# A decoder trunk's attention stage: the order of TensorE's products written out by hand

## The chip, the cores and the metric

The kernel runs on one core of a Trainium2 chip. The metric is the device time of one execution in microseconds, as the median of several runs; less is better. The engines of the core work in parallel, each on its own queue of instructions and in the order of that queue: TensorE (PE; matrix products and transposes by a product with the identity), VectorE (DVE), ScalarE (ACT), GpSimd (POOL, which here also issues the gathers), and SyncE (SP), which issues other transfers.

## The reference

Two layers of a decoder: an mLSTM mixer, then multi-head latent attention, each followed by a SwiGLU block. It is computed for a prompt of 1,024 tokens and for 8 decode streams with one new token and 8,192 cached keys each. The change lies in the attention of the second layer:

```python
def mla_attend_prompt(q_lat, q_rope, c_kv, k_r):           # per block of queries, causal
    s = jnp.einsum('bqhc,bkc->bhqk', ql, c_kv) + jnp.einsum('bqhr,bkr->bhqk', qr, k_r)
    s = jnp.where(kpos[None, :] <= qpos[:, None], s * MLA_SCALE, -jnp.inf)
    p = jax.nn.softmax(s, axis=-1)
    return jnp.einsum('bhqk,bkc->bqhc', p, c_kv)

def mla_attend_sample(q_lat, q_rope, c_new, kr_new, cache_latent, cache_k_rope, page_table, layer_idx):
    def one_seq(args):                                     # per stream: all 8192 past keys and the new one
        c_all = jnp.concatenate([cache_latent[layer_idx, pages].reshape(past, KV_LORA), cn], axis=0)
        s = jnp.einsum('qhc,kc->hqk', ql, c_all) + jnp.einsum('qhr,kr->hqk', qr, kr_all)
        p = jax.nn.softmax(jnp.where(mask, s * MLA_SCALE, -jnp.inf), axis=-1)
        return jnp.einsum('hqk,kc->qhc', p, c_all)
```

There are 8 heads, 256 latent channels and 64 rotary ones; everything is float32, and the prompt's products are each made of three, from a high and a low part of both operands.

## The kernel before

**Prompt blocks and slots.** The prompt's attention is cut into 32 blocks, one per head `h` and group `G` of 256 queries; block (h, G) has 2G + 2 tiles of 128 keys, so `G` = 0 is short and `G` = 3 long. Block number 4h + i is a *slot* (i counts up to 3 in a head; odd heads but the last go through `G` from 3 down). In `prompt(h, G, ...)` TensorE makes two rows of scores `sc` (L1529 to L1536: three products with the keys `kt`, two with the rotary keys, a mask), DVE finds their maxima `mx` (L1537), ACT takes the exponentials into `px` (tag `wr`, L1546) and scales them by the reciprocal of their sum (L1551; from slot `LATE` on DVE does). Then TensorE *turns* the scaled tiles by products with the identity (L1567, into an `mm` bank), ACT and POOL split them into high and low parts `wh` and `wl` (L125 to L127, through a copy `spl`), the last turn of a block by ACT and DVE (L114, L115), and the *values* are the products with `vt` (L1587). `head_ops(h + 1)` makes the next head's `kt`, and for even heads the `vt` of two heads, a piece per slot (L131 to L133).

**Key halves.** The streams' cached keys come in 32 pieces of 2,048 keys; one is called a *half*, two make a unit, two units a stream. POOL gathers a half's latent rows into `nat` (four buffers, two gathers of 1 MB each) and its rotary rows into `nrp` (two buffers). DVE transposes them in five passes into `tt` (four buffers, L1684), and TensorE makes the stream's scores from each `tt`, 32 columns at a time (L1691; `qbd` holds the queries). After two halves comes the unit's softmax: maximum `rm` and bias `nb` on DVE, `al` and the exponentials `sS` on ACT (L1700, L1704), the running sum `lrow` and the transpose `pT` on DVE, sixteen copies of `pT` into `pz`, half on DVE and half on ACT (L1712), and the *stream sum* on TensorE, 32 products of `nat` by `pz` in the source, which read `nat` for the last time (L1716); `acc` takes it up. After a stream's second unit its *meeting* follows: ten small steps between DVE, TensorE and ACT that bring the keys' partial maxima and sums together (L1722 to L1741).

**What sets the order.** The source writes, slot by slot, a whole prompt block, a piece of `head_ops`, and one half (two in the slots `DBL`, none in `NONE`) from the generator `sample_units`. A scheduler then orders each engine's instructions by their priority, which is the place in the source, and by when it expects their operands; stream scores and sums are raised by `high_priority(offset=SOON)`. The queues' order is fixed when the program is built; at run time an engine only waits. `mmt(tag)` takes one of eight PSUM banks: four `sc`, two `mm`, two `ss`.

## Time and profile before

| | |
|---|---|
| median of 3 runs | 2774.49 us (2773.03 to 2780.6) |
| the profiled execution's own time | 2772.8 us |
| its span, first to last instruction | 2771.0 us |
| mean granted TensorE clock | 0.971 |
| busy: PE, DVE, ACT, POOL | 2594.2, 1497.7, 1177.0, 875.5 us |
| instructions in the profile | 52011 |

In the profile, lines as L1691 are those of the listing above. A group of instructions shows its busy time and the mean duration in ns, then the idle time of its engine just before, and what ended it. A row of waits shows who waited for whom, the total in us, the times and the longest. A float32 product shows as two PE instructions where the source has one. Slots 1 to 29 lie between about 1411 and 1907 us of the span, the stream work between 1435 and 1904.

### The profile page before, as it was taken

The numbers are of one execution on the slowest core, as the hardware profiler recorded it, in microseconds if no ns is written. First come the engines' busy times: TensorE is split into PE (matmuls) and PEld (weight loads), VectorE is DVE, ScalarE is ACT, GpSimd is POOL, SyncE is SP. The second block draws the span as 40 slices with busy tenths as digits, with TensorE's granted clock in tenths as the row PEclk, the third lists the DMA queues.
The fourth block names the chain that finished last, engine by engine and source line by source line (L and its number), as shares of the span: only waits on it lengthen the run. The fifth ranks groups of instructions, "written<-read, shape, count | busy, mean of one in ns | idle before, by whom it ended". The sixth has DMA issues, their size and how long they took to land. (4 is left out here: it accounts for less than half of the span.)

```text
span 2771.0 us, 52011 instructions
## 1 busy us (share of the span) xinstructions
PE 2594.2 (94%) x20719; PEld 2445.1 (88%) x20719; DVE 1497.7 (54%) x3217; ACT 1177.0 (42%) x2651; POOL 875.5 (32%) x843
## 2 busy tenths in 40 slices
PE   8999988989999999999878889898988999999998
PEld 8998877889999999998766677676888999999998
DVE  4345678853344333465547776677574444434445
ACT  4212334534444444443353455456344444444443
POOL 1001002243333333332243545442223333333333
PEclk9999999999999999999988999899999999999999
DMA  5133445326655656463566766653533655555553
GB/s 184 39 76 92 132 144 147 116 79 129 121 117 117 119 120 117 84 195 108 173 210 220 259 228 228 223 204 125 174 100 85 127 117 120 120 117 117 117 134 106
DMA packets 348905, 383.70 MB, mean 138 GB/s; under 512 B 26025, under 2 KB 300462, under 8 KB 340342
## 3 DMA queue, kind: packets, MB, share of 16 engines
q0 software_dynamic: 42064, 180.99, 27.7%
q1 hardware_dynamic: 279654, 182.83, 22.5%
q10 hardware_dynamic: 26944, 16.56, 2.3%
q8 instruction: 163, 2.67, 0.4%
q14 instruction: 80, 0.66, 0.1%
HBM read 254.58 MB, written 125.70 MB: 137 GB/s over the span
## 5 line engine op out<-in xcount | busy, mean ns | idle before, releaser
L131 PE MATMUL ss<-ah,dh 128*128 128x344 f32 x864 | 277.4, 321 | 6.6 <-ACT st L1075 6.2
L1075 ACT COPY st<-ss 128x344 f32<-128x344 f32 x432 | 189.9, 441 | 213.3 <-PE ss L133 180.4
L132 PE MATMUL ss<-al,dh 128*128 128x344 f32 x864 | 277.3, 321 | 1.9 <-POOL al L115 1.9
L133 PE MATMUL ss<-ah,dl 128*128 128x344 f32 x864 | 276.6, 320 | 0.0
L114 ACT ACTIVATE wh<-wr 128x512 fp32r<-128x512 f32 (+2 forms) x161 | 130.7, 812 | 238.7 <-PE mm L132 130.5
L1077 POOL DMA_DIRECT2D x_d<-st x144 | 124.3, 863 | 243.7 <-ACT st L1075 237.8
L131 PEld LDWEIGHTS ss<-ah,dh 128*128 128x128 f32 x864 | 163.0, 189 | 7.6 <-ACT st L1075 6.7
L132 PEld LDWEIGHTS ss<-al,dh 128*128 128x128 f32 x864 | 163.3, 189 | 2.4 <-POOL al L115 2.4
L115 POOL TENSOR_TENSOR al<-u,ah 128x512 fp32r<-128x512 f32 (+1 forms) x84 | 118.2, 1407 | 147.8 <-ACT ah L114 147.6
L1684 DVE STREAM_TRANSPOSE tt<-nat 128x1024 f32<-128x1024 f32 x128 | 153.8, 1223 | 18.9 <-PE ss L1691 13.8
L133 PEld LDWEIGHTS ss<-ah,dl 128*128 128x128 f32 x864 | 162.9, 189 | 0.0
L115 DVE TENSOR_TENSOR wl<-S,wl 128x512 fp32r<-128x512 f32 x89 | 77.4, 870 | 157.3 <-ACT wl L114 122.8
L115 DVE TENSOR_TENSOR wh<-S,wh 128x512 fp32r<-128x512 f32 x91 | 68.2, 750 | 121.5 <-ACT wh L114 93.1
L1041 DVE TENSOR_TENSOR u<-u,sc 128x260 f32<-128x260 f32 (+1 forms) x168 | 70.8, 422 | 115.0 <-PE sc L133 113.7
L115 DVE TENSOR_TENSOR wl<-wr,wh 128x1024 fp32r<-128x1024 f32 (+2 forms) x92 | 105.2, 1143 | 50.0 <-ACT wh L114 42.4
L1691 PE MATMUL ss<-tt,qbd 128*32 128x128 f32 x2560 | 99.0, 288 | 21.7 <-DVE tt L1684 12.8
L1007 POOL TENSOR_TENSOR S<-S,wr 128x512 f32<-128x512 f32 x45 | 62.9, 1397 | 175.8 <-DVE wl L115 87.9
L1000 POOL TENSOR_TENSOR S<-wr 128x512 f32<-128x512 f32 x45 | 61.6, 1369 | 163.4 <-DMA wr<-in_ffn_w_gate_up_dram 153.9
L1691 PEld LDWEIGHTS ss<-tt,qbd 128*32 128x32 f32 x2560 | 75.3, 114 | 40.4 <-DVE tt L1684 21.0
L131 PE MATMUL mm<-zh,wh 128*128 128x344 f32 x320 | 104.0, 325 | 7.2 <-DVE ot L459 7.2
L115 DVE TENSOR_TENSOR dl<-dr,dh 128x256 fp32r<-128x256 f32 x144 | 68.6, 476 | 72.9 <-ACT dh L114 72.9
L132 PE MATMUL mm<-zl,wh 128*128 128x344 f32 x320 | 103.2, 322 | 0.0
(917 smaller groups left out, 9275.8 us busy)
## 6 DMA issues: line engine op xcount, KB each, us to landing
x_d<-st POOLq DMA_DIRECT2D x144, 516.0 KB
wr<-in_ffn_w_gate_up_dram SPq DMA_DIRECT2D x98, 512.0 KB
dr<-in_ffn_w_down_dram SPq DMA_DIRECT2D x144, 128.0 KB
wr<-in_mlstm_w_in_dram SPq DMA_DIRECT2D x24, 512.0 KB
wr<-in_mlstm_w_out_dram SPq DMA_DIRECT2D x16, 512.0 KB
q<-qn_d SPq DMA_DIRECT2D x32, 256.0 KB
wr<-in_mla_w_o_dram SPq DMA_DIRECT2D x15, 512.0 KB
x_d<-x SPq DMA_DIRECT2D x16, 260.0 KB
```

What stands on the lines that cost most here:

```text
L114: ins = nc.scalar.activation(hi, src, AF.Copy)
L115: self.low = e.tensor_tensor(lo, src, hi.bitcast(F32), op=ALU.subtract)
L131: mm(ps, wh, xh, start=start, stop=False, **kw)
L132: mm(ps, wh, xl, start=False, stop=False, **kw)
L133: self.last = mm(ps, wl, xh, start=False, stop=stop, **kw)
L1000: G(s, a21, a22, op=ALU.add)
L1007: G(s, s, a11, op=ALU.subtract)
L1041: V.tensor_tensor(u[:, 1], u[:, 1], ps, op=ALU.add)
L1075: nc.scalar.copy(st[:, cs], ps)
L1077: nc.gpsimd.dma_start(self.x_d[:, d], st, accum_op=ALU.add)
L1684: V.transpose(out=tt, in_=src.rearrange("p s (c i) -> p c s i", i=32))
L1691: nc.tensor.matmul(psS[32 * j:32 * j + 32, u * P:u * P + P], self.qbd[:, b, cb], tt[:, c, 4 * j:4 * j + 4].rearrange("p s k -> p (s k)"), ...
```

## The change

The generator `sample_units`, the generator `head_ops` and the function `prompt` become objects with small steps: `Sample` (all streams), `Half` (one half), `Block` (one slot's prompt block). For slots 1 to 29 one loop writes the steps of both in a fixed pattern, and after the loop every TensorE instruction written in it gets a dependency on the TensorE instruction written before, without a semaphore: TensorE's queue is in the source's order. The other engines' queues are still the scheduler's. In the pattern of a slot:

- the *next* block's two rows of scores and their scaling are written in this slot (`nxt.scores`, `nxt.scale`), with this block's turns ahead and between them, two turns to a group, and its values at the end;
- a half's stream scores come in two groups, of three tiles at the slot's start and of two behind the next block's first scores; its transposes are written up to a half ahead;
- a unit's softmax is written at the end of its second half, its `pT` in the next half behind three transposes, its stream sum ahead of that slot's values; twelve of the sixteen `pz` copies are ACT's;
- a freed `nat` is gathered again right behind the sum (one now, one with the next half), `nrp` two halves ahead, and a block's `q` is loaded two slots ahead;
- a meeting's ten steps are spread as *hops* over the following halves, in the unit's own `ss` bank;
- the next head's keys and values are made in `sc` banks instead of `mm`; `DBL` is (4, 12, 20) and `NONE` is empty; `high_priority` is gone.

The core of the diff:

```diff
-NONE, DBL, LATE = (0, 31, 30), (3, 11, 27), 30
-SOON = 1000
+NONE, DBL, LATE = (), (4, 12, 20), 30
...
+    def probs(self):
+        if self.todo:
+            d = self.units[self.todo[0]]
+            if "pT" in d and not d.get("pz"):
+                for kb in range(4):
+                    for j in range(4):
+                        e = self.V.tensor_copy if kb == 3 else self.nc.scalar.copy
+                        e(self.k.pz[32 * kb:32 * kb + 32, j, :, 8 * kb:8 * kb + 8], d["pT"][32 * j:32 * j + 32, kb])
+                d["pz"] = True
+    def sums(self):
+        if not self.todo:
+            return False
+        U = self.todo[0]
+        d = self.units[U]
+        if not d.get("pz"):
+            return False
+        self.todo.pop(0)
+        nc, V = self.nc, self.V
+        psV = d["ss"][:, 256:512]
+        for i in range(8):
+            for j in range(4):
+                nc.tensor.matmul(psV[32 * j:32 * j + 32], self.k.pz[:, j, i], self.nat[2 * U + i // 4][:, j * 4 + i % 4], start=i == 0, stop=i == 7)
+        self.gather(2 * U + 4)
+        self.due = 2 * U + 5
+        self.add = lambda: V.scalar_tensor_tensor(d["q"]["acc"], d["q"]["acc"], d["al"], psV, op0=ALU.mult, op1=ALU.add)
+        return True
...
+    def soft(self, U):
+        nc, V, t = self.nc, self.V, self.t
+        d = self.units[U]
+        q = d["q"]
+        psS = d["ss"][:, 0:256]
+        rm = t([P, 1], "rm", 2)
+        V.reduce_max(rm, psS, axis=AX.X)
+        nb = t([P, 1], "nb", 3)
+        V.scalar_tensor_tensor(nb, rm, -SCALE, q["nb"], op0=ALU.mult, op1=ALU.min)
+        al = d["al"] = t([P, 1], "al", 2)
+        nc.scalar.activation(al, q["nb"], AF.Exp, bias=nb, scale=-1.0)
+        q["nb"] = nb
+        d["sS"] = t([P, 256], "sS", 1)
+        d["ls"] = t([P, 1], "ls", 2)
+        nc.scalar.activation(d["sS"], psS, AF.Exp, bias=nb, scale=SCALE, accum_out=d["ls"])
+        self.wait = U
+    def soft2(self, U):
+        V, t = self.V, self.t
+        d = self.units[U]
+        q = d["q"]
+        V.scalar_tensor_tensor(q["lrow"], q["lrow"], d["al"], d["ls"], op0=ALU.mult, op1=ALU.add)
+        d["pT"] = t([P, 4, 8, 8], "pT", 1)
+        V.transpose(out=d["pT"].rearrange("p k t h -> p t k h"), in_=d["sS"])
+        self.todo.append(U)
+        if U % 2:
+            self.meet(U)
...
+        s.scores(u, (1, 4, 0))
+        s.fetch()
+        s.turn(u, 2)
+        s.turn(u, 3)
+        s.turn(u + 1, 4)
+        s.late()
+        s.hop("V")
+    def second(self):
+        s, u = self.s, self.u
+        s.hop("P")
+        s.turn(u + 1, 0)
+        s.scores(u, (3, 2))
+        s.hop("V")
+    def third(self):
+        self.s.turn(self.u + 1, 1)
+    def fourth(self):
+        s, u = self.s, self.u
+        if u % 2:
+            s.soft(self.U)
+        s.rope(u + 2)
...
-            for i, G in enumerate(range(4) if h % 2 == 0 or h == 7 else range(3, -1, -1)):
-                slot = h * 4 + i
-                if slot >= early:
-                    prompt(h, G, cur["k"], vt)
-                next(gen, None)
-                if pr is None:
-                    pr = self.pr = self.pool("ma")
-                for _ in range(0 if slot in NONE else 2 if slot in DBL else 1):
-                    next(units)
...
+        for slot in range(1, 30):
+            h, i = divmod(slot, 4)
+            halves = [sam.take() for _ in range(0 if slot in NONE else 2 if slot in DBL else 1)]
+            u = halves[0] if halves else sam
+            far = Block(slot + 2)
+            far.load()
+            u.first()
+            ups = []
+            if h % 2 == 0 and h < 7:
+                if i == 0 and h > 0:
+                    ups = [lambda: make_v(h, 3, split_p, "sc"), lambda: load_uk(h + 1)]
+                if i == 2:
+                    ups = [lambda: make_k(h + 1, split_p, "sc"), lambda: load_uk(h + 2) if h < 6 else None]
+            elif h < 7:
+                if i == 0:
+                    ups = [lambda: make_k(h + 1, split_p, "sc"), lambda: load_uv(h + 1)]
+                else:
+                    ups = [lambda: make_v(h + 1, i - 1, split_p, "sc")]
+            turns = [lambda j=j: blk.turn(j) for j in range(0, blk.nk, 2)]
+            seq = turns[:2] + ups + turns[2:3] if full or not ups else ups + turns[:2]
+            rest = turns[len([x for x in seq if x in turns]):]
+            for f in seq:
+                f()
+            nxt.scores(0)
+            for f in rest[:1]:
+                f()
+            if len(halves) > 1:
+                sam.probs()
+                u.second()
+                for f in rest[1:]:
+                    f()
+                nxt.scale(0)
+                sam.sums()
+                u.third()
+                nxt.scores(1)
+                sam.hop("P")
+                u.fourth()
+                u = halves[1]
+                u.first()
+                sam.probs()
+                nxt.scale(1)
+                blk.values()
+                u.second()
+                full = sam.sums()
+            else:
+                sam.probs()
+                u.second()
+                for f in rest[1:]:
+                    f()
+                nxt.scale(0)
+                nxt.scores(1)
+                full = sam.sums()
+                nxt.scale(1)
+                blk.values()
+            u.third()
+            sam.hop("P")
+            u.fourth()
+            blk, nxt = nxt, far
...
+        traced = nc.cur_bb.bb.instructions
+        mark = traced[-1]
...
+        last = {}
+        for ins in traced[[k for k in range(len(traced)) if traced[k] is mark][-1] + 1:]:
+            e = ins.engine
+            if e == mybir.EngineType.PE and e in last:
+                self.tc.add_manual_dep(ins, last[e].name, mybir.DependencyInfo(mybir.DependencyClass.NoSync, mybir.DependencyReason.DATA), reason="order")
+            last[e] = ins
```

The order before and after, in slot 17 (head 4, `G` = 1, a block of four key tiles). On TensorE, before; `mm_18067` is a value tile of the next heads, `mm_18259` a turn of the slot's predecessor, `sc_18579` this block's scores, `ss_18300` the stream scores of a unit, `mm_18267` values:

```order
L132 MATMUL mm_18067<-swl_17699,ckh_13605 128x256
L133 MATMUL mm_18067<-swh_17697,ckl_13606 128x256
L1567 MATMUL mm_18259<-ct_66,wr_18238 128x128
L1567 MATMUL mm_18259<-ct_66,wr_18253 128x128 x2
L1529 MATMUL sc_18579<-kt_17555,q_18573 128x384
L1691 MATMUL ss_18300<-tt_18494,qbd_15149 32x128 x8
L1691 MATMUL ss_18300<-tt_18492,qbd_15149 32x128 x8
L1587 MATMUL mm_18267<-wh_18257,vt_16233 128x256
L1530 MATMUL sc_18579<-kt_17555,q_18573 128x384
L1531 MATMUL sc_18579<-kt_17555,q_18573 128x384
L1532 MATMUL sc_18579<-kk_13597,qrr_18574 128x384
```

After, from the same block's start; `ss_18547` holds stream scores, `mm_18586` and `mm_18595` are this block's two turns, and `sc_18605` the scores of slot 18:

```order
L143 MATMUL ss_18547<-tt_18526,qbd_15149 32x128 x8
L143 MATMUL ss_18547<-tt_18429,qbd_15149 32x128 x8
L143 MATMUL ss_18547<-tt_18479,qbd_15149 32x128 x8
L1832 MATMUL mm_18586<-ct_66,wr_18476 128x128
L1832 MATMUL mm_18586<-ct_66,wr_18512 128x128
L1832 MATMUL mm_18586<-ct_66,wr_18476 128x128
L1832 MATMUL mm_18586<-ct_66,wr_18512 128x128
L1832 MATMUL mm_18595<-ct_66,wr_18476 128x128
L1832 MATMUL mm_18595<-ct_66,wr_18512 128x128 x2
L1789 MATMUL sc_18605<-kt_17535,q_18394 128x512
```

Before, stream scores cut a value tile's six-product chain and the block's scores, and each kind of product follows another after one to three instructions; now each kind runs to its end, and the block that is scored is the next one.

On ACT, the softmax of the unit whose sum stands in slot 17 (`sS_18518` before, `sS_18536` after), with the prompt's exponentials and scales (`wr_...,sm_...` from `sc`, then `wr` from `wr`). Before:

```order
L1551 ACTIVATE wr_18410<-wr_18410,sm_18400 128x256
L1700 ACTIVATE al_18516<-nb_15151,nb_18514 128x1
L1704 ACTIVATE sS_18518,ls_18519<-ss_18300,nb_18514 128x256
L1590 COPY ot_18274<-mm_18267 128x256
L1592 DMA ot_d_14312<-ot_18274 128x256
L1712 COPY pz_14408<-pT_18522 32x8x8 x8
L125 ACTIVATE vt_18277<-mm_18278 128x512
L126 COPY spl_18291<-mm_18278 128x512
```

After:

```order
L1806 ACTIVATE wr_18512,sm_18502<-sc_18503,mx_18501,rqt_14290 128x512
L224 ACTIVATE al_18534<-nb_15151,nb_18532 128x1
L228 ACTIVATE sS_18536,ls_18537<-ss_18203,nb_18532 128x256
L1816 ACTIVATE wr_18512<-wr_18512,sm_18502 128x512
L379 ACTIVATE wh_18584<-mm_18586 128x512
L380 COPY spl_18591<-mm_18586 128x512
L368 ACTIVATE wh_18584<-mm_18595 128x256
L158 COPY pz_14408<-pT_18582 32x8x8 x11
L368 ACTIVATE wh_18584<-mm_18595 128x128
L158 COPY pz_14408<-pT_18582 32x8x8
```

The scale of the block that is turned next (`wr_18512`) now stands behind the unit's `al` and `sS`, and twelve `pz` copies, instead of eight, follow the splits of that block's turns.

On DVE, the transposes about the same unit's `pT`. Before:

```order
L1696 TENSOR_REDUCE rm_18512<-ss_18300 128x1
L115 TENSOR_TENSOR wl_18258<-mm_18259,wh_18257 128x128
L1698 SCALAR_TENSOR_TENSOR nb_18514<-rm_18512,nb_15151 128x1
L1537 TENSOR_REDUCE mx_18577<-sc_18579 128x1
L1684 STREAM_TRANSPOSE tt_18653<-nat_18643 128x1024
L1705 SCALAR_TENSOR_TENSOR lrow_18298<-lrow_18298,al_18516,ls_18519 128x1
L1707 STREAM_TRANSPOSE pT_18522<-sS_18518 128x8x4x8
L1543 TENSOR_SCALAR mx_18577<-mx_18577,rqt_14290 128x1
L1712 COPY pz_14408<-pT_18522 32x8x8 x8
L1684 STREAM_TRANSPOSE tt_18679<-nat_18643 128x1024
```

After:

```order
L134 STREAM_TRANSPOSE tt_18575<-nat_18371 128x1024
L1814 RECIPROCAL sm_18502<-sm_18502 128x1
L134 STREAM_TRANSPOSE tt_18577<-nat_18371 128x1024
L134 STREAM_TRANSPOSE tt_18579<-nrp_18539 128x1024
L235 SCALAR_TENSOR_TENSOR lrow_18204<-lrow_18204,al_18534,ls_18537 128x1
L237 STREAM_TRANSPOSE pT_18582<-sS_18536 128x8x4x8
L134 STREAM_TRANSPOSE tt_18640<-nat_18422 128x1024
L369 TENSOR_TENSOR wl_18585<-mm_18595,wh_18584 128x256
L1797 TENSOR_REDUCE mx_18603<-sc_18605 128x1
L369 TENSOR_TENSOR wl_18585<-mm_18595,wh_18584 128x128
L1797 TENSOR_REDUCE mx_18603<-sc_18612 128x1
L158 COPY pz_14408<-pT_18582 32x8x8 x2
```

Before, one `tt` transpose stood between the unit's bias `nb` and its `pT`, and the eight copies came right behind; now three transposes stand ahead of `pT`, and one more, with the next block's maxima and a split, between it and the four copies.

On POOL, a unit's `nat` gathers and the splits about them. Before:

```order
L1676 DMA nat_18301<-in_cache_latent_dram,idx_13601 128x2048 x2
L127 TENSOR_TENSOR wl_17609<-spl_17615,wh_17608 128x512
L127 TENSOR_TENSOR wl_17609<-spl_17624,wh_17608 128x512
L1676 DMA nat_18456<-in_cache_latent_dram,idx_13601 128x2048
L127 TENSOR_TENSOR wl_17629<-spl_17635,wh_17628 128x512
L1676 DMA nat_18456<-in_cache_latent_dram,idx_13601 128x2048
L1677 DMA nrp_18457<-in_cache_k_rope_dram,idx_13601 128x512
```

After:

```order
L381 TENSOR_TENSOR wl_18585<-spl_18591,wh_18584 128x512
L117 DMA nrp_18935<-in_cache_k_rope_dram,idx_13601 128x512
L117 DMA nat_18714<-in_cache_latent_dram,idx_13601 128x2048 x2
L117 DMA nat_18769<-in_cache_latent_dram,idx_13601 128x2048 x2
L381 TENSOR_TENSOR wl_18780<-spl_18786,wh_18779 128x512
L381 TENSOR_TENSOR wl_18780<-spl_18795,wh_18779 128x512
L117 DMA nrp_19175<-in_cache_k_rope_dram,idx_13601 128x512
```

Both tiles that the sum in slot 17 frees are gathered in a row, ahead of the splits of slot 18's turns (`wl_18780`).

466 lines of the change are left out of this document (260 added, 206 removed).

## The prediction

> **What bounds the kernel now.** I read the page first: busy shares, the slices, then the waits of TensorE in the stage that the diff touches.
>
> ```profile
> PE 2594.2 (94%) x20719; PEld 2445.1 (88%) x20719; DVE 1497.7 (54%) x3217; ACT 1177.0 (42%) x2651; POOL 875.5 (32%) x843
> PE   8999988989999999999878889898988999999998
> PEclk9999999999999999999988999899999999999999
> ```
>
> TensorE is the bound (94%), and the attention stage, slices 21 to 28, is where its digits and its clock dip. The view by windows cuts out the stretch from the first stream score to the end of the last stream sum, with the 41 us behind it; the columns are PE, PEld, DVE, ACT, POOL busy, then granted clock and DMA share.
>
> ```profile
> 1447.00:1902.00 455.00, 397.61 (x4953) 314.78 (x4953) 329.02 (x700) 225.58 (x600) 202.18 (x198) 0.92 0.63 218
> 1902.00:1943.00 41.00, 34.87 (x191) 29.41 (x190) 28.12 (x66) 25.60 (x70) 16.29 (x25) 0.88 0.59 192
> ```
>
> 455 us are 397.6 of busy TensorE and 57.4 of waiting. At the granted 0.92 the busy part is 366 us of full-clock work (397.6 x 0.92), so the clock costs 32 us. No other engine is near full: DVE, the next, has 329 us (72%). The view of waits says what TensorE waited for there (us, times, longest):
>
> ```profile
> PE ss L1691 <- DVE tt L1684: 12.8, 11, 2.4
> PE ss L1716 <- ACT pz L1712: 8.8, 9, 2.7
> PE ss L1691 <- issue: 7.7, 17, 1.1
> PE mm L1587 <- ACT spl L126: 5.2, 8, 1.4
> PE mm L1587 <- DVE wl L115: 4.7, 3, 2.9
> PE mm L1567 <- ACT spl L126: 4.7, 7, 1.0
> ```
>
> Many short waits of about a microsecond, spread over stream scores (tiles not yet transposed), stream sums (`pz` not yet copied) and the prompt's turns and values (splits not done). All are of the kind that another order can cover, except the 7.7 us of "issue", which no product's readiness explains; I leave those.
>
> **The change, part by part.** *Fewer changes between kinds of product.* In the order of before, TensorE goes from one output tile to another 489 times between the first stream score and the last sum; in the order of after 337 times: 152 fewer. The timeline gives the price: a 512-wide product starts 0.23 us after its like, but 0.32 us (1440.56 to 1440.88, and 1441.87 to 1442.19) when it follows a turn.
>
> ```profile
> 1573.32 0.39 PE L132 MATMUL mm<-ckl,swh 128*128 128x512 f32 x1
> 1573.55 0.39 PE L133 MATMUL mm<-ckh,swl 128*128 128x512 f32 x1
> ...
> 1440.56 0.48 PE L1529 MATMUL sc<-kt,q 128*128 128x512 f32 x1
> 1440.88 0.40 PE L1530 MATMUL sc<-kt,q 128*128 128x512 f32 x1
> 1441.13 0.98 PE L1567 MATMUL mm<-ct,wr 128*128 128x128 f32 x7
> 1441.87 0.48 PE L1531 MATMUL sc<-kt,q 128*128 128x512 f32 x1
> 1442.19 0.39 PE L1532 MATMUL sc<-kk,qrr 128*128 128x512 f32 x1
> ```
>
> 0.09 us x 152 = 13 us of full-clock work; 366 becomes 353. Ends: 0 (the row is a worst case) and 25 (a change into the 32-column stream products may cost twice that). I take 13, the row itself.
>
> *The waits.* I work out four neighbouring key halves of the new order by hand (slots 15 to 18), from these durations:
>
> ```profile
> 1565.26 1.08 PE L1691 MATMUL ss<-tt,qbd 128*32 128x128 f32 x32
> 1568.91 1.52 PE L1691 MATMUL ss<-tt,qbd 128*32 128x128 f32 x48
> 1599.71 3.91 PE L1716 MATMUL ss<-nat,pz 128*32 128x256 f32 x64 [0.28 <-ACT pz L1712]
> 1571.65 0.69 DVE L1537 TENSOR_REDUCE mx<-sc 128x1 f32<-128x512 f32 x1 [0.16 <-PE sc L1536]
> 1575.14 3.48 DVE L1684 STREAM_TRANSPOSE tt<-nat 128x1024 f32<-128x1024 f32 x3
> 1578.65 0.43 DVE L1707 STREAM_TRANSPOSE pT<-sS 128x256 f32<-128x256 f32 x1
> 1573.62 0.78 ACT L1546 ACTIVATE wr<-sc,mx,rqt 128x512 f32<-128x512 f32 x1
> 1574.30 0.19 ACT L1546 ACTIVATION_READ_ACCUMULATOR wr<-sc,mx,rqt 128x1 f32 x1
> 1575.64 0.74 ACT L1551 ACTIVATE wr<-wr,sm 128x512 f32<-128x512 f32 x1
> 1577.21 0.32 ACT L1700 ACTIVATE al<-nb,nb 128x1 f32<-128x1 f32 x1
> 1577.40 0.49 ACT L1704 ACTIVATE sS<-ss,nb 128x256 f32<-128x256 f32 x1
> 1578.46 0.60 ACT L125 ACTIVATE wh<-mm 128x512 fp32r<-128x512 f32 x1 [0.47 <-PE mm L1567]
> 1578.95 0.58 ACT L126 COPY spl<-mm 128x512 f32<-128x512 f32 x1
> 1579.56 1.01 ACT L1712 COPY pz<-pT 32x64 f32<-32x64 f32 x4
> ```
>
> Slot 17 (a block of two key pairs, with a stream sum), clock at 0 with its first stream scores, 1.5 us: the last prompt scores of slot 16 ended at -0.9 (six value products and a meeting's two stand between), their maximum (0.7, with a stream reduce and small steps behind it) is out at 0.5, and ACT then runs in its new order exp, `al`, `sS`, scale: 0.8 + 0.2 + 0.3 + 0.7 (with an accumulator read) + 0.7 brings the scaled block at 3.2 to 3.3. The turns wait 1.8 us for it. Seven turns (0.8), the next block's scores (1,408 columns in five products each, 3.3 at 0.23 per 512), the second stream scores (1.1) and 0.3 for the changes between them then end at 8.9. DVE has three transposes (1.2 each) ahead of `pT`, which is out at 5.3; twelve `pz` copies of 0.25 us on ACT, behind the splits of the turns (0.6 each), end at 8.7, and DVE's four at 9.4, since a transpose and two maxima stand ahead of them. The sum waits 0.5 us. Slot 18 (a key product of 2.8 us, no sum): 0.2 us. Slot 15 (one key pair, a sum): a `pz` copy stands ahead of the scale on ACT, so the turn comes 2.6 us late. Slot 16: 0.6 us. That is 5.8 us in four halves.
>
> Over 32 halves: 16 have a sum; in the four with 2.8 us of key products or a long block ahead of it nothing waits, in twelve about 2.1 us, together 25. The other 16 wait 0.4, together 6. In the light halves (one key pair, 6 to 8 us of TensorE) DVE's five transposes and two maxima are longer than TensorE's work; I give 6 us. The "issue" waits stay, 8. I add 4 us for what I don't see: 49 us against 57. Ends: 20 us (8 of issue and 0.7 in every second half) and 80 us (2.9 in all 16 sum halves, 0.7 in the others, 8 of issue, and 0.9 x 16 for gathers a little late).
>
> *The clock.* It falls in this stage after short stalls. The same 32 stream products took 1.08 us above and 1.94 us here, behind a few microseconds in which TensorE had waited again and again for tiles:
>
> ```profile
> 1592.04 1.94 PE L1691 MATMUL ss<-tt,qbd 128*32 128x128 f32 x32 [0.44 <-DVE tt L1684]
> ```
>
> With 49 instead of 57 us of waits I take 0.93 for 0.92: 353 / 0.93 = 380 us busy, 18 less than 397.6 (14 of it from the changes of product, 4 from the clock). Ends: 0.90 (392) and 0.95 (372). The Trainium skill (TensorE: Matmul & The Clock Gate, Part 1, What's actually happening) has the clock halve only after an idle window of about 3.4 us. By that the clock would stay full through waits of 2.9 us and less, its term would be 0, and the sum 2747. The trace does not agree: 0.92 was granted over 455 us whose longest TensorE wait is 2.9 us.
>
> *ACT takes four `pz` copies more per unit, DVE four fewer*: 4 x 16 x 0.25 = 16 us more on ACT. ACT's free time covers it (225.6 busy of 455); where that cover is gone, before a sum, it is in the waits above.
>
> *Queues.* Loads of `q` are issued two slots ahead on SP, and `nrp` gathers two halves ahead on POOL, each into a buffer that was read a slot before: 0, hidden by a slot of some 14 us; without that cover one exposed load is 6 us (the row at 1424.85 below). The gather of `nat` now stands on POOL right behind the sum that frees its buffer, ahead of the next slot's splits, which aren't ready sooner: 0, if it lands in time (third rival). Key and value products take `sc` banks: two of four are held for two splits of 1.2 us on ACT while the scores ahead need the other two: 0; exposed, 7 x 2.4 = 17 us. The meetings' steps keep their number; DVE waited for them, TensorE did not: 0.
>
> *Start and end.* The new order puts stream scores ahead of block 1's turns, so TensorE must wait for the first gather.
>
> ```profile
> 1412.13 1.07 POOL L1676 DMA_INDIRECT nat<-in_cache_latent_dram,idx  x1 [3.07 <-PE ss L1411]
> 1424.85 0.80 PE L1529 MATMUL sc<-kt,q 128*128 128x512 f32 x1 [6.22 <-DMA q<-qn_d]
> 1431.86 1.29 POOL L127 TENSOR_TENSOR kt<-spl,kt 128x512 fp32r<-128x512 f32 x1 [18.66 <-ACT spl L126]
> 1447.62 2.06 PE L1691 MATMUL ss<-tt,qbd 128*32 128x128 f32 x48 [2.22 <-DVE tt L1684]
> ```
>
> Before, gathers stood behind a split that POOL awaited for 18.7 us; now twelve gather issues come first, from about 1412, so the first scores can run near 1425 to 1430, when `q` arrives anyway. What TensorE did before 1447.6 (two blocks) it does later, and the stream work earlier: 0, with ends of -6 and +6. At the end the scores of block 30 are done before the last sum instead of behind it, and the 41 us behind it shrink by about 5 (0 to 10).
>
> **Sum**, against the profiled execution's 2772.8 us (span 2771.0; 1.7 under the median of 2774.5): -18 busy, -8 waits, 0 start, -5 end = -31: **2742 us**.
>
> **Rivals.**
> - *TensorE is nearly fed* (waits 20 us, clock 0.95): -26 - 37 - 5 = -68, 2705 us. For it: none of the covered waits is long. Against: my four halves show new ones.
> - *Fewer but longer waits cost clock.* Each of 13 waits above 2 us is followed by a slow spell like that from 1592.0, where 32 products lost 0.9 us, and the spell about 1.6 in all: 13 x 1.6 = 21, so 2763 us. For it: 0.92 with waits under 3 us. Against: the waits before were as long.
> - *Late gathers (slower).* A freed `nat` is now wanted sooner: behind the sum come twelve value products (1.4 at half of 0.23 each), two tiles' stream scores (1.0) and two transposes (2.4), 4.8 us, and the first gather is issued 1.9 us ahead of the sum's end: 6.7 us in all.
>
> ```profile
> 1585.08 0.95 POOL L1676 DMA_INDIRECT nat<-in_cache_latent_dram,idx  x1 [1.80 <-PE ss L1716]
> 1590.74 1.25 DVE L1684 STREAM_TRANSPOSE tt<-nat 128x1024 f32<-128x1024 f32 x1 [3.06 <-remote]
> ```
>
> It landed in 5.7 us, 1.0 to spare. DVE takes its queue in order, so a late tile holds up the maxima, the exponentials and the next turns. Landing in 9.5 us costs 2.8 x 16 = 45: 2787 us; from 8.6 us on (31 / 16 beyond the spare) nothing is gained. For it: the stage's DMA share of 0.63 rises with a shorter stage. Against: the 5.7 us were measured with four such gathers on their way.
> - *Nothing moves*: the other engines' chains set the pace (DVE 72% busy, in order), TensorE's order only shifts its waits: 2772 us.
>
> **How the numbers follow.** Forecast 0.50, fed 0.17, clock 0.13, gathers 0.13, nothing 0.07. 0.3% (8.3 us) is about what a measurement of this kernel tells from no change. Faster: nearly all of the first, the second, half of the third, 0.71; same: 0.13; slower: the gathers and the worst of the rest, 0.16. The range reaches from the fed case with the start's -6 (2699) to just short of the late gathers (2784); the likeliest case alone spans 2713 to 2773, by the ends of its widest term, the waits.
>
> **What would show it.** Right: the stage's busy TensorE near 380 us, waits near 50, clock 0.93; "PE ss <- ACT pz" above its 8.8 us, "PE mm <- ACT wr" (turns awaiting the scale, not among the waits above) over 10, and the waits of values for splits nearly gone. The fed case shows waits under 30; the clock case 0.90 or less; the gathers show as DVE waiting "remote" or on DMA, over 30 us. The prediction is wrong if the other engines' order, which a scheduler still sets, holds a block back by more than the 0.2 to 2.6 us worked out.

## The result, and the profile after

The changed kernel took 2782.11 us (median of 20 runs, 2770.83 to 2792.37) against 2774.69 us for the kernel before (20 runs, 2764.01 to 2782.71): a ratio of 1.0031, 95% interval 1.0021 to 1.004. It is 7 us slower where 31 us less were forecast. The profiled execution is the longest of the 20: 2792.4 us, with a span of 2790.4.

The page of the changed kernel, its busy shares and the rows of TensorE and its clock over the span:

```profile
PE 2600.4 (93%) x20719; PEld 2458.1 (88%) x20719; DVE 1493.9 (54%) x3153; ACT 1195.0 (43%) x2715; POOL 874.5 (31%) x843
PE   8999988889999999999877888888988999999998
PEclk9999989999999999999978999998999999999999
```

The digits of TensorE in slices 21 to 28 are lower than before (7 and 8 where 8 and 9 stood). Part of the 19.4 us between the two profiled spans lies outside the attention, so I measure one *stretch* in every profile: from block 0's first prompt score to the first `sc` product of the output projection behind its 24 `mm` products. By windows, before and then after (columns as in the prediction):

```profile
1403.40:1952.00 548.60, 473.98 (x5356) 377.83 (x5355) 372.12 (x807) 278.80 (x733) 235.55 (x241) 0.91 0.63 216
```

```profile
1412.40:1963.10 550.70, 463.25 (x5356) 377.25 (x5355) 365.37 (x743) 296.05 (x797) 232.42 (x237) 0.91 0.59 209
```

The stretch is 2.1 us longer: 10.7 us less of busy TensorE, and 12.8 us more of waiting (87.4 against 74.6). Ahead of it lie 9.0 us more in this pair of profiles, behind it 8.3; in the later profiles, of all kernels, the part ahead came out between 1407 and 1416 us and the part behind between 817 and 824, so I take no conclusion from those two. TensorE's waits from the first to the last stream work, after:

```profile
PE ss L143 <- issue: 12.0, 25, 1.0
PE ss L173 <- ACT pz L158: 11.2, 6, 5.5
PE mm L1832 <- ACT wr L1816: 9.1, 4, 3.5
PE ss L143 <- DVE tt L134: 8.6, 2, 7.6
PE mm L1854 <- ACT wh L368: 7.9, 2, 3.9
PE mm L1832 <- ACT spl L380: 7.7, 8, 2.6
PE ss L143 <- DVE olat L282: 5.9, 6, 1.8
PE mm L1854 <- DVE wl L369: 4.6, 5, 1.2
PE ss L279 <- DVE w L275: 3.2, 2, 1.7
```

Waits of transposed tiles are nearly gone: of 8.6 us, 7.6 are the first gather. In their place stand fewer and longer ones for ScalarE's part of the prompt (`wr` scaled, `wh` split) and for the steps of the meetings, which had cost TensorE 0.7 us before.

The same pair of kernels was then profiled on two other Trainium2 chips, where the kernel before is 30 us faster (2743 us), and there the loss is plain. The stretch of the kernel before, and of the changed one:

```profile
1409.50:1922.10 512.60, 452.75 (x5357) 364.97 (x5356) 368.72 (x807) 278.47 (x734) 235.71 (x240) 0.94 0.67 230
```

```profile
1413.40:1953.60 540.20, 457.70 (x5357) 379.68 (x5356) 360.32 (x743) 295.86 (x797) 232.28 (x237) 0.90 0.60 213
```

27.6 us more: 22.6 of waiting and 5 of busy TensorE, at a clock of 0.90 for 0.94. VectorE's waits on the transfers of the latent tiles in these two profiles, before and then after:

```profile
DVE tt L1684 <- DMA nat<-in_cache_latent_dram,idx: 3.2, 5, 1.5
```

```profile
DVE tt L134 <- DMA nat<-in_cache_latent_dram,idx: 29.1, 13, 3.4
```

On the first chip the same wait is far smaller, in the changed kernel too (its first profile; the kernel before has no such row there):

```profile
DVE tt L134 <- remote: 11.8, 4, 3.3
DVE tt L134 <- DMA nat<-in_cache_latent_dram,idx: 5.6, 7, 1.2
```

The four waits that end on "remote" are no transfers: each of these transposes waits on TensorE's semaphore, for a `tt` buffer that stream scores are still reading.

One of the 13 waits on the faster kind of chip, in the timeline of the changed kernel (rows of other instructions left out):

```profile
1541.22 0.97 POOL L117 DMA_INDIRECT nat<-in_cache_latent_dram,idx  x1 [0.49 <-PE ss L173]
...
1542.49 0.95 POOL L117 DMA_INDIRECT nat<-in_cache_latent_dram,idx  x1 [0.30 <-issue]
...
1543.75 0.95 POOL L117 DMA_INDIRECT nat<-in_cache_latent_dram,idx  x1 [0.30 <-issue]
...
1545.01 0.95 POOL L117 DMA_INDIRECT nat<-in_cache_latent_dram,idx  x1 [0.31 <-PE ss L143]
...
1551.50 1.25 DVE L134 STREAM_TRANSPOSE tt<-nat 128x1024 f32<-128x1024 f32 x1 [3.42 <-DMA nat<-in_cache_latent_dram,idx]
...
1552.67 0.25 DVE L1797 TENSOR_REDUCE mx<-sc 128x1 f32<-128x128 f32 x1
...
1554.12 1.08 PE L143 MATMUL ss<-tt,qbd 128*32 128x128 f32 x32 [3.46 <-DVE tt L134]
1554.20 0.46 ACT L1806 ACTIVATE wr<-sc,mx,rqt 128x128 f32<-128x128 f32 x1 [5.48 <-DVE mx L1803]
```

The sum frees two tiles at 1541.2; the first is wanted at 1548.1, and can be read at 1551.5, 10.3 us after its gather was issued. VectorE takes its queue in order, so the next block's maximum stands behind, ScalarE waits 5.5 us for it, and TensorE stands 3.5 us. From here I call the time from the issue of a unit's first freed tile's gather to that tile's first transpose its *age*: over the 14 units in this profile it is 8.9 to 10.3 us, with a wait on the transfer in 13; in the kernel before on the same kind of chip it is 9.0 to 35.4 us (half of them 12 or more), with a wait of over 0.3 us in four.

### The profile page after: what moved, and what is told of

Read it like the earlier page. It is cut to its first block, busy times and chain, and to the rows that moved or that the text cites. A ratio compares the mean times of both kernels' runs of the same rounds, so it can differ in the third digit from the quotient of the medians.

```text
span 2790.4 us, 51988 instructions
## 1 busy us (share of the span) xinstructions
PE 2600.4 (93%) x20719; PEld 2458.1 (88%) x20719; DVE 1493.9 (54%) x3153; ACT 1195.0 (43%) x2715; POOL 874.5 (31%) x843
## 4 chain that ended last, share of the span: by engine, by line
PE 66%; DVE 12%; DMA 9%; issue 6%; ACT 4%; POOL 3%; SPq 0%; another core or an unknown queue 0%; ACTq 0%; POOLq 0%; DVEq 0%
PE sc L385 10%; PE sc L387 9%; PE sc L386 9%; PE mm L385 5%; PE ss L385 5%; PE ss L386 5%; PE ss L387 5%; PE mm L386 5%; PE mm L387 5%; PE ss L173 2%; DMA Gb<-G_d 2%; PE ss L143 1%; DVE wl L369 1%; DVE tt L134 1%; DMA nat<-in_cache_latent_dram,idx 1%
## 5 line engine op out<-in xcount | busy, mean ns | idle before, releaser
L369 DVE TENSOR_TENSOR wl<-wr,wh 128x1024 fp32r<-128x1024 f32 (+2 forms) x92 | 105.6, 1148 | 58.4 <-ACT wh L368 50.7
L143 PE MATMUL ss<-tt,qbd 128*32 128x128 f32 x2560 | 99.7, 287 | 27.6 <-issue 12.0
```

The source lines that it names most:

```text
L143: self.nc.tensor.matmul(ps[32 * j:32 * j + 32], self.k.qbd[:, u // 4, cb], tt[:, c, 4 * j:4 * j + 4].rearrange("p s k -> p (s k)"), start= ...
L369: self.low = e.tensor_tensor(lo, src, hi.bitcast(F32), op=ALU.subtract)
```

## The experiments

The table has all that was measured; `ratio` is to the kernel before on the same chip, with its 95% interval, stretch and TensorE's figures are from each kernel's profile (waiting is stretch less busy).

| kernel | us | before | ratio | stretch | busy | waiting | clock |
|---|---|---|---|---|---|---|---|
| changed, again | 2775.9 | 2744.1 | 1.0115 (1.01 to 1.0131) | 540.2 | 457.7 | 82.5 | 0.90 |
| act_fixed | 2833.9 | 2744.1 | 1.0328 (1.031 to 1.0346) | 600.4 | 477.3 | 123.1 | 0.87 |
| act_dve_fixed | 2800.1 | 2744.1 | 1.0208 (1.0191 to 1.0225) | 566.3 | 461.1 | 105.2 | 0.90 |
| pe_free | 2761.4 | 2744.1 | 1.0062 (1.0049 to 1.0076) | 541.6 | 462.3 | 79.3 | 0.91 |
| before_again | 2742.7 | 2743.2 | 0.9993 (0.9978 to 1.0009) | 512.6 | 452.8 | 59.9 | 0.94 |
| start_late | 2776.5 | 2743.2 | 1.0124 (1.0105 to 1.0142) | 542.2 | 458.0 | 84.2 | 0.89 |
| hops_early | 2786.5 | 2743.2 | 1.0159 (1.0134 to 1.0183) | 546.3 | 456.8 | 89.5 | 0.90 |
| pz_all_act | 2779.3 | 2743.2 | 1.0118 (1.01 to 1.0137) | 551.2 | 463.8 | 87.5 | 0.89 |
| no_regather | 2737.6 | 2773.8 | 0.9877 (0.986 to 0.9895) | 492.7 | 433.0 | 59.7 | 0.94 |
| before_no_regather | 2749.1 | 2773.8 | 0.9915 (0.99 to 0.993) | 511.0 | 455.2 | 55.8 | 0.93 |
| second_tile_late | 2794.7 | 2773.8 | 1.009 (1.0068 to 1.0112) | 558.5 | 462.9 | 95.6 | 0.91 |
| pool_fixed | 2851.3 | 2773.8 | 1.0276 (1.0259 to 1.0293) | 619.1 | 495.9 | 123.3 | 0.86 |
| changed_control | 2782.9 | 2773.0 | 1.0029 (1.0012 to 1.0046) | 541.1 | 459.8 | 81.3 | 0.92 |
| second_tile_behind | 2782.5 | 2773.0 | 1.0026 (1.0012 to 1.0041) | 550.2 | 458.0 | 92.2 | 0.91 |
| second_tile_behind_free | 2773.8 | 2773.0 | 1.0005 (0.9987 to 1.0024) | 540.3 | 459.1 | 81.2 | 0.92 |
| no_regather_free | 2721.6 | 2773.0 | 0.9808 (0.9782 to 0.9834) | 485.4 | 438.8 | 46.6 | 0.96 |
| transposes_late | 2793.3 | 2771.0 | 1.0087 (1.0069 to 1.0105) | 555.0 | 461.1 | 93.9 | 0.89 |
| transposes_late_free | 2756.1 | 2771.0 | 0.9957 (0.9937 to 0.9977) | 518.4 | 456.3 | 62.1 | 0.93 |

Chips come in two kinds here, by the kernel before: 2743 and 2771 to 2775 us. A ratio is therefore compared only with one on the same kind.

### The changed kernel and the one before, once more

> The changed kernel once more, unedited, for a second profile of it. The measure used below is the attention stretch, from the first prompt score of block 0 to the product of the output projection that follows its first 24 products in a row: 548.6 us before and 550.7 us after in the two profiles so far, so 2 of the 19.4 us between those profiles. If the loss lies in the attention, this profile has 551 to 558 us there, and the time is 2778 to 2786 us. If the loss of the 20 runs came from elsewhere, the stretch is 545 to 550 us.

> The kernel before once more, unedited, for a second profile of it, beside the kernels of this study. On the chip of the first four runs it took 2744 us, 31 less than in the profile shown, and the changed kernel 2776. If the attention carries the difference, its stretch is 515 to 525 us here (the parts ahead of it and behind it took 1403 and 819 us in the profile shown); if those parts do, it is 540 to 549.

> The changed kernel unedited, as the control of the three others on one chip: a stretch of 540 to 551 us, and 0.3 to 1.2 per cent above the kernel before, by the chip.

The attention carries the loss on the faster kind of chip: 512.6 against 540.2 us of stretch. The first is just under the kernel before's first alternative, the second under both lines expected for the changed kernel. On the slower kind the changed kernel is as it was (541.1, and 550.7 in the first profile) and the kernel before is 36 us longer. The changed kernel barely feels the difference of the chips, the kernel before does; why, is open (below).

### Which queues are fixed

The edit in each: the engines whose instructions are chained in the loop behind the 29 steps.

```diff
-            if e == mybir.EngineType.PE and e in last:
+            if e in (mybir.EngineType.PE, mybir.EngineType.Activation) and e in last:   # act_fixed; act_dve_fixed adds DVE
+            if False and e in last:                                                     # pe_free
```

> ScalarE's queue is put in the source's order too, in the 29 steps. Theory 1 (the queues of the other engines, which the scheduler still orders, hold the fixed TensorE up): the values' wait for the last split, 8.9 us over 3 waits, and the turns' wait for the scaled block, 9.1 us, nearly go; the stretch is 8 to 15 us shorter than the changed kernel's, 536 to 543 us. Theory 2 (the chains through DVE and ScalarE are as long in any order): the waits change their names, the stretch stays at 547 to 555. A loss beyond that would say that the scheduler's order of ScalarE was the better one.

> ScalarE's and VectorE's queues are both put in the source's order. Theory 1: as much as with ScalarE alone or more, stretch 530 to 543 us, since the maxima and the running sums then stand where the source has them. Theory 2: 547 to 555. Against both: in the source's order a queue waits for the first operand that is late, so each late gather or score holds up everything behind it; then it is slower than 555.

> The loop that chains TensorE's instructions is taken out; source and steps are the same, and the scheduler orders TensorE too. Theory 3 (fixing TensorE's order is itself the loss, since it may not take a ready product): the stretch falls to 535 to 543 us. Theories 1 and 2: the new source order carries the change, and without the chain the scheduler brings back the mixed order; products change kind more often (10 us more of busy time), the stretch is 548 to 560 us.

Theory 1 falls. With ScalarE in the source's order the stretch grows by 60 us; its profile shows what for:

```profile
PE ss L173 <- ACT pz L158: 47.9, 14, 6.8
PE mm L1854 <- ACT wh L368: 19.0, 7, 6.2
```

The stream sum waits for the `pz` copies, and those for what stands ahead of them on ScalarE. Its own longest waits in that profile:

```profile
ACT wh L368 <- DVE wl L369: 50.2, 29, 8.0
ACT wr L1806 <- DVE mx L1801: 46.3, 14, 8.0
```

In the second profile of the changed kernel these two are 13.1 and 23.8 us. For `pT` itself ScalarE waits 0.7 us: in the source's order it stands for VectorE's low parts and maxima. With VectorE's queue in the source's order as well the stretch is 566.3 us, slower than both theories say. The scheduler's order of the other engines was the better one. Without the chain on TensorE the time is 14.5 us less (1.0062 against 1.0115, intervals apart), although its stretch is not shorter in the one profile (of the longest of its five executions): TensorE stood there 20.7 us for a load of `q` issued during the twelve first gathers, once, and less everywhere else. So on this kind of chip the fixed order is part of the loss, and not all of it.

### Three suspected waits, each by itself

> In slot 1 alone the first stream scores are written behind block 1's first turns and the first scores of block 2, instead of ahead of them. Theory 4 (the new start is a loss: TensorE stands 7.6 to 8.1 us for the first gathered tile, with turns and scores ready behind it): the wait goes nearly whole, the stretch is 5 to 8 us shorter than the changed kernel's 540.2 (second profile). Rival: the stream work is what the whole stage is paced by, a later start of it is paid back later; the stretch stays within 2 us.

```diff
-            u.first()
+            if slot > 1:
+                u.first()
...
             nxt.scores(0)
+            if slot == 1:
+                u.first()
```

The rival: the stretch is 542.2 us, not shorter. TensorE's early wait is given back, since stream work then starts 8 us later (30.3 us behind the first prompt score for 22.5).

> Two more places for a meeting's steps, behind the next block's second scores in slots with one half, so that the last steps are done half a slot before the next unit wants the ss bank. Theory 5 (the spread meetings hold the ss bank and TensorE stands for their small steps: stream scores behind olat 6.8, products of w 7.1, of m 2.0 and lrow 0.6 us, 16.5 in all in the second profile): those waits fall below 8 us and the stretch is 5 to 9 us shorter. Rival: the steps only come before a VectorE that is just as late; the waits keep their sum within 3 us.

```diff
                 nxt.scores(1)
+                sam.hop("P")
+                sam.hop("V")
                 full = sam.sums()
```

Neither: the stream scores' wait for `olat` fell from 6.8 to 2.3 us, but the products with `w` (10.1 us) and with the maxima (8.6) together waited 18.7 us for VectorE's small steps where they had waited 7.1, and the stretch is 6 us longer. In a fixed queue an earlier place for a small product is a longer wait.

> All sixteen pz copies are ScalarE's, none VectorE's. Theory 6 (a pz copy on VectorE that meets a row of GpSimd's splits stands until the row is over: copies of 5.5, 5.6 and 3.2 us in the first profile of the changed kernel, 0.19 else, with the block's maxima behind them): no such copy, 14 us less on VectorE, and 3 to 8 us off the stretch. Rival: four copies of 0.24 us more on ScalarE for each of 16 sums, 15 us, lie on the path to the sum and to the next scaled block; the stretch is 5 to 10 us longer.

```diff
-                        e = self.V.tensor_copy if kb == 3 else self.nc.scalar.copy
+                        e = self.nc.scalar.copy
```

Nothing gained: 1.0118, with 11 us more of stretch in its profile. The stuck copies were real (last section) and went, 27 us less of VectorE's busy time, and the sum waited longer for ScalarE's copies instead (10.6 us for 5.8).

### The gathers left out

> The changed kernel with the four nat tiles gathered once and then read again in their turn: no latent gather behind a sum, the rotary gathers stay (the streams' keys are thus the first four halves over and over). Theory 7 (late gathers, the prediction's slower rival): in the second profile of the changed kernel VectorE waits 29.1 us for nat tiles, up to 3.4 us behind nearly every sum, 9 to 10 us after the first of four gathers was issued, with the block's maxima behind it. Without them the stretch falls from 540 to 512 to 522 us. Rival (the chains through VectorE and ScalarE and the fixed order itself): the stretch falls by 8 us or less.

> The kernel before with the same left out. Its second profile shows 3.2 us of VectorE waiting for nat, so both theories expect little: a stretch of 505 to 512 us (512.6 with gathers). If theory 7 is the whole loss, the changed kernel without gathers is then at or below this one; if it is none of it, it stays some 25 us above.

```diff
-        if u < 32:
+        if u < 4:
             self.nat[u] = self.t([P, 16, 256], "nat", 4)
             self.load(u, self.nat[u], self.k.cache_latent)
+        elif u < 32:
+            self.nat[u] = self.nat[u - 4]
```

The stretch of the changed order, and then that of the order before, without the later latent gathers:

```profile
1412.40:1905.10 492.70, 433.03 (x5356) 355.08 (x5355) 349.54 (x743) 296.80 (x797) 179.72 (x183) 0.94 0.36 115
```

```profile
1408.40:1919.40 511.00, 455.18 (x5355) 360.48 (x5355) 371.55 (x807) 278.72 (x733) 180.34 (x183) 0.93 0.37 115
```

Without the later gathers the changed order is the better one, by 18.3 us of stretch and 11.5 us of time (0.9877 against 0.9915, intervals apart): the direction that the prediction forecast, at about a third of its 31 us. With them it loses. So the gathers turn the sign. (The 492.7 us lie below the 512 to 522 expected, which were reckoned from the faster kind of chip.)

Both kernels pay for them on this kind of chip. The changed one pays about 48 us of stretch (541.1 of `changed_control` less 492.7, on two chips) and 1.5% of time; the kernel before pays 38 us (548.6 of its first profile less 511.0) and 0.85%, where both theories had expected little. What the gathers take from the change here is the difference, 0.67% or 19 us. And these two runs leave out all that comes with a gather: its issue, its transfer and the wait for it. They don't show that the wait is what costs.

### Why the tiles are late

> GpSimd's queue is put in the source's order, with both gathers where they were: what the kernel with the later second tile has beside it. Either theory: within 5 us of the changed kernel's 540, as the four gathers stay together and only the rotary gathers and the splits change places.

> GpSimd's queue is put in the source's order too, and the second freed tile is gathered behind the next slot's splits instead of right behind the first one. Theory 7: the first tile, which is wanted first, then has the transfer rate for itself and lands in 6 to 7 us instead of 9 to 10; VectorE's wait for nat falls below 12 us and the stretch to 520 to 532. Rival: the wait only moves to the second tile, or the splits wait for the gathers ahead of them; the stretch stays at 537 to 550.

In the first, GpSimd's queue was chained like TensorE's; in the second, `s.fetch()` also stands behind the second stream scores instead of at the half's start. The control is no control: fixing that queue costs 78 us of stretch, and GpSimd's splits then wait longer for what ScalarE copies for them (91.0 us for 50.7 in the `wl` split, 75.4 for 25.1 in the `vt` one), with everything written behind them. The later second tile gave 60 of the 78 back, and 558.5 us lies outside both lines expected. Nothing follows for the changed kernel but that the second tile's place matters in such a queue, so it was moved alone:

> Only the second tile's two gathers are moved: in GpSimd's queue they follow the splits that the source has ahead of them in the next slot, a few microseconds later than the first tile's; the rest of that queue stays the scheduler's. Theory 7 (four gathers in a row share the transfer rate, so the tile wanted first lands in 9 to 10 us): the first tile lands in 6 to 7 us, VectorE's wait for nat falls from 17 to 29 us to below 12, and the stretch is 10 to 20 us shorter than the control's. Rival (the turn-around is too short however the gathers stand, or the second tile is then as late): the stretch is within 5 us of the control's.

```diff
-            if e == mybir.EngineType.PE and e in last:
+            if e in last and (e == mybir.EngineType.PE or e == mybir.EngineType.Pool and ins.name in sam.held):
```

(`held` has the second tile's gathers, and `s.fetch()` stands where it stood in `second_tile_late`.) The rival holds, the time is the control's. The first tile's age is 8.7 to 10.0 us with, as a rule, only its own two latent gathers on their way, as it was with four: that the four share the rate is not why it is late. The second tile is now as late; in the timeline of this kernel its two gathers, and its first transpose 10.2 us after the first of them:

```profile
1622.96 0.97 POOL L117 DMA_INDIRECT nat<-in_cache_latent_dram,idx  x1 [0.16 <-issue]
1624.23 0.95 POOL L117 DMA_INDIRECT nat<-in_cache_latent_dram,idx  x1 [0.31 <-issue]
```

```profile
1633.11 1.25 DVE L136 STREAM_TRANSPOSE tt<-nat 128x1024 f32<-128x1024 f32 x1 [2.82 <-DMA nat<-in_cache_latent_dram,idx]
```

So a tile of 2 MB takes 9 to 10 us from its issue, and the new order wants it after 7.

> The same, and TensorE's order is the scheduler's again. Theory 3 (the fixed order is itself a loss): another 10 us or more off. Rival (the fixed order pays once the tiles come in time): 5 to 15 us longer than with the fixed order, by the products that change kind more often and by the 20.7 us that TensorE stood for q at the start of the first kernel without the chain.

> The four nat tiles are gathered once and read again in their turn, and TensorE's order is the scheduler's: beside the kernel that leaves the gathers out with the fixed order (492.7 us of stretch) it prices the fixed order alone. Theory 3: below 488 us. Rival: 495 to 510 us.

With the gathers out, TensorE's order left to the scheduler is better by 7.3 us of stretch and by 0.7% (0.9808 against 0.9877, intervals apart): theory 3, also where no tile is late. With the gathers and the second tile behind, the free order has 9.9 us less of stretch, but the intervals of 1.0005 and 1.0026 overlap.

### The transposes moved, and a version that beats both

> In the odd halves the next tile's first two transposes are written behind the next block's scores and scaling instead of ahead of them, and held there in VectorE's queue, so that a tile that lands 9 to 10 us after its gather no longer stands ahead of the block's maxima; TensorE's order is unchanged. Theory 8 (the turn-around: the new order wants a freed tile 6.7 us after the gather's issue, and a late one blocks VectorE's queue): VectorE's wait for nat falls below 8 us, the waits of values and turns for ScalarE shrink, the stretch is 10 to 20 us shorter than 541, against 2.5 us more in some of the 16 odd halves' ends where the stream scores wait for the two transposes. Rival: the scores at the next half's start then wait for the transposes in every odd half, 3 us x 16 = 48 us, and it is slower than the changed kernel.

> The same with TensorE's order left to the scheduler. Theory 3 (the fixed order is a loss of 7 to 15 us): 7 to 15 us less than with the fixed order. With theory 8 as well this one is below the kernel before: a ratio of 0.985 to 0.997. Rival: as slow as the kernel with TensorE free and the gathers as they were, 1.005 or more on a chip where the kernel before takes 2744 us, 1.000 where it takes 2773.

```diff
-        s.turn(u + 1, 0)                               # in second()
+        if u % 2 == 0:
+            s.turn(u + 1, 0)
...
-        self.s.turn(self.u + 1, 1)                     # in third()
+        if self.u % 2:
+            self.s.turn(self.u + 1, 0, True)           # True: held behind VectorE's instruction written before it
+        self.s.turn(self.u + 1, 1, self.u % 2 == 1)
```

TensorE's wait for transposed tiles with the fixed order, and then with TensorE's order free:

```profile
PE ss L145 <- DVE tt L134: 37.6, 8, 7.5
```

```profile
PE ss L145 <- DVE tt L134: 11.1, 10, 3.5
```

In both, no wait of VectorE's on a latent tile's transfer is left. In the fixed queue that buys nothing: the scores at the next half's start wait for the late transposes, 37.6 us, as the rival had it, and it is slower than the changed kernel. With TensorE free the queue holds other work there: 518.4 us of stretch and 0.9957 (0.9937 to 0.9977), 2756.1 against 2771.0 us for the kernel before on that chip. On this kind of chip, the slower one, this version beats both; it was not run on the faster. Between the two stand 37 us, the price of the fixed order in this place (7 to 15 were expected). It is also the nearest that the runs come to pricing the late tile alone: in `second_tile_behind_free`, with TensorE free and as many gathers, VectorE waited 28.8 us for tiles and the ratio was 1.0005 (0.9987 to 1.0024). The 0.5% between the two go with that wait, though the second tile's place differs as well.

## Why the prediction was wrong, step by step

Two steps failed, and cost about as much each. Between the 31 us less that were forecast and the 7 more that were measured lie 38 us. Some 20 of them are missing without the later gathers too (11.5 us less, not 31), and 19 of those come back when TensorE's order is left to the scheduler (0.9877 and 0.9808): that is the waits in the fixed queue, forecast to shrink. The other 19 come with the gathers, which were put at 0. Both figures are differences of ratios from several chips of the slower kind, good to some 7 us.

**Fewer changes of product: right.** Forecast 14 us less of busy TensorE for them, 13 at full clock; the stretch has 10.7 less on the first chip, 5.0 more on the faster kind, where the clock fell, and without gathers 22 less (455.2 and 433.0). Busy time multiplied by the granted clock gives an estimate of the work at full clock: 10, 14 and 16 us less in the three pairs. Leaving TensorE's order to the scheduler brings 9 to 14 us of it back, by the same estimate, in the changed kernel, without gathers and with the transposes late.

**The waits: the first step that failed, wrong in sign.** Forecast 49 us between first and last stream work for 57; measured 74.9, by the window of those 485 us (30 us more than the window of before, since the stream work starts earlier):

```profile
1435.00:1920.00 485.00, 410.09 (x5052) 334.21 (x5053) 331.54 (x665) 261.17 (x710) 206.30 (x202) 0.93 0.59 208
```

The named signs came partly: `pz` 11.2 us (said: above 8.8), turns awaiting the scale 9.1 (said: over 10). But the values' waits for splits, "nearly gone", are 14.7 us (7.9, 4.6, 2.2), where 13.0 stood: the scheduler puts the last turn's split behind the next block's exponentials on ScalarE, which wait for VectorE. And meetings at "0, TensorE did not wait for them" were wrong: in a fixed queue it waits for their steps, 11.1 us (`olat` 5.9, `w` 3.2, `m` 2.0). Without the later gathers the stretch still has 59.7 us of waiting for 55.8, so this step fails by itself.

**The gathers: the second step that failed.** "0, if it lands in time", with a landing of 5.7 us read from one row against a need of 6.7. The need was about right: age less wait is 6.1 to 8.9 us (median 7.3) in the second profile of the changed kernel. The landing was not a landing. The row at 1590.74 reads another tile than the one that was gathered at 1585.08. A half's tile is transposed in four passes, and its rotary rows in a fifth; the row is the fourth pass over the tile gathered here:

```profile
1560.86 0.95 POOL L1676 DMA_INDIRECT nat<-in_cache_latent_dram,idx  x1 [0.30 <-issue]
1562.11 0.94 POOL L1676 DMA_INDIRECT nat<-in_cache_latent_dram,idx  x1 [0.30 <-issue]
...
1583.78 3.49 DVE L1684 STREAM_TRANSPOSE tt<-nat 128x1024 f32<-128x1024 f32 x3
...
1591.91 1.20 DVE L1684 STREAM_TRANSPOSE tt<-nrp 128x1024 f32<-128x1024 f32 x1
```

The tile gathered from 1585.08 on was first transposed at 1599.06, and the last of its packets in the trace, counted in order, ended at 1593.05. And the row's wait ended by "remote", no transfer; it waits on TensorE's semaphore, for the `tt` buffer that the stream products were still reading. They stood at that moment, in the kernel before:

```profile
1587.85 0.38 PE L1691 MATMUL ss<-tt,qbd 128*32 128x128 f32 x3 [0.32 <-issue]
1588.57 0.41 PE L1691 MATMUL ss<-tt,qbd 128*32 128x128 f32 x4 [0.35 <-issue]
...
1589.28 0.43 PE L1691 MATMUL ss<-tt,qbd 128*32 128x128 f32 x6 [0.30 <-issue]
1590.70 0.41 PE L1691 MATMUL ss<-tt,qbd 128*32 128x128 f32 x3 [0.99 <-issue]
```

Rows that do end on the transfer stand 8.9 to 10.3 us behind the issue (second profile). The third rival had that landing (9.5 us), and was given a chance of 0.13 on the strength of a spare 1.0 us that did not exist. That its sum, 45 us of loss and 2787 us, comes near the 2782 measured is in good part luck. It counts 2.8 us for each of 16 tiles, but in the first profile VectorE waits 5.6 us for transfers in all, and the sign it named, over 30 us on "remote" or DMA, read 17.4; on the faster kind it read 29.1. And the gathers are only half of the shortfall. How much of their 19 us on the slower kind is the late tile, and how much TensorE's "issue" waits beside the transfers (last section), wasn't separated.

The Trainium skill (DMA: Bandwidth & Descriptors, Anatomy of one DMA — SWDGE (gpsimd) path) puts a transfer that GpSimd issues at about 2.0 us and its bytes at 436 GB/s; for two of 1 MB in a row that is an estimate of 6.8 us from the first, which already leaves nothing of a need of 6.7. The runs have 9 to 10.

**The clock.** Forecast 0.93 for 0.92 in the stage: it was 0.93 (the row above), and 0.91 for 0.91 over the stretch. Where the waits grew most, on the faster chips, it fell from 0.94 to 0.90 with 15 waits of over 2 us for 6; that is the second rival's mechanism beside the third's. What it alone cost wasn't separated. No long wait is needed for it: in the kernel before the granted clock was 0.50 from 1591.9 to 1595.3 us, behind 4.8 us (1587.0 to 1591.8) in which TensorE was busy for 2.6 and never waited more than 1.0 at a time.

**Start and end.** The start is a wash, as forecast: stream scores begin 22.8 us behind the first prompt score instead of 44.2, at 7.6 us of waiting, and moving it changed nothing. From the last sum to the end of the stretch it is 38.9 us for 50.0, 11 less where 5 (0 to 10) were forecast.

**What the forecast had no step for.** The fixed order itself, which I priced at the changes it saves. Each wait in it is a wait of everything behind. Taken off, it gave 0.5% in the changed kernel, 0.7% without gathers and 1.3% with the transposes late, net of the changes of product that came back. The new source with neither the later gathers nor the fixed order is 1.1% or 30 us below the kernel before without them (0.9808 and 0.9915): about the 31 us forecast, but not by the order that the forecast priced.

Still open: why the kernel before, and not the changed one, gains 36 us of stretch on the faster chips. The runs give a hint: on the slower kind and without the later gathers it has 511.0 us, nearly its 512.6 with them on the faster kind. So the two kinds may differ in what gathers cost this kernel; without a run that leaves them out on the faster kind this isn't shown.

## What to carry to other kernels

Read a transfer's landing from a wait that ends on that transfer, and make sure that the row reads the buffer which that transfer filled; a wait that ends on anything else says nothing of it. When you leave something out to price it, leave it out of the kernel before as well: here it, too, had paid. When buffers are fewer than the reuse needs, the time from the release of a buffer to its next reading is a term of its own: a new order that releases it as late and reads it half a stage earlier has to pay for the transfer, and on an engine whose queue is in order it pays with all that is queued behind. A queue fixed by hand is worth its saved changes of product only when nearly every operand comes in time; here the same source with the queue left to the scheduler was better in every pair whose intervals lie apart.

## What the runs showed of the hardware that was not expected

A copy of 0.19 us on VectorE can stand for 5.6 us behind GpSimd's splits. In the first profile of the changed kernel, four `pz` copies on VectorE, and GpSimd's rows at that time:

```profile
1592.51 6.24 DVE L158 COPY pz<-pT 32x64 f32<-32x64 f32 x4
```

```profile
1593.45 2.54 POOL L381 TENSOR_TENSOR kt<-spl,kt 128x512 fp32r<-128x512 f32 x2
1595.94 2.53 POOL L381 TENSOR_TENSOR wl<-spl,wh 128x512 fp32r<-128x512 f32 x2
```

The copies end 0.3 us behind the last split. Three of the 64 copies took 3.2, 5.5 and 5.6 us, each beside a row of splits; in the kernel before, where splits stand singly or in twos, seldom in threes, the longest of 128 was 1.3. The Trainium skill (SBUF — State Buffer, SBUF: two separate sides) says that the two engines share a port pair, which one instruction holds whole while the other blocks, where VectorE's is of a kind that uses the pair, as a float32 copy within SBUF is. The trace agrees, and here the copy didn't get in between four splits that follow each other at once. That is not always so: in the kernel before, two copies of 1.2 us each ran beside two such splits (from 1875.6 on), and the first ended as the second split began.

On the slower kind of chip TensorE's stream scores wait for "issue" while gathers are issued and under way: 12.0 us in the first profile of the changed kernel (rows of up to 1.0 us), 7.7 in the kernel before, and 2.7 or none in the kernels without the later gathers. On the faster kind no profile shows such a wait. What they wait for the profile doesn't show.
